# Small TensorE products grouped in a planned order: hybrid retention, hgrn2 and differential attention, two layers

## The chip, the cores and the metric

One Trainium2 chip, one of its cores. The metric is the device time of one execution in microseconds (us). The kernel before was run three times; the median is 1280.63 us.

## The reference

Two layers over 272 tokens (16 learned "meta" tokens and 256 of the input), width 1024, float32. Each layer normalizes the tokens, multiplies them by one wide matrix `w_in` and hands the columns to three branches: retention, hgrn2 and differential attention. Each branch output passes its own 1024 x 1024 matrix, is gated by a sigmoid and summed; `w_out` follows, then a feed-forward block with a three-tap convolution. Cut to what matters here:

```python
proj = (hn @ w_in).astype(F32)
rq, rk, rv, rg, hq, hf, hi, hg, dq, dk, dv, mg = jnp.split(proj, offs, axis=-1)
o_ret = retention(rq, rk, rv, rg, ...)        # 4 heads, s = (q k) * decay, o = s v, rms, * silu(rg)
o_hg  = hgrn2(hq, hf, hi, hg, lb, valid)      # 8 heads, a[q,k] = sum_d q k exp(cb_q - cb_k), o = a v
o_da  = diff_attention(dq, dk, dv, ...)       # 8 heads, w = softmax_0 - lam * softmax_1, o = w v
y = sum over the three of sigmoid(mg) * (branch @ w_branch)
h = h + y @ w_out
h = h + (silu(gate) * val) @ w_ffn_out        # gate, val from a convolution of h @ w_ffn_in
```

## The kernel before, in words

**The main products.** Tokens stand along the free dimension (272 columns; 258 in the last layer, where the first 14 meta tokens are needed for keys and values only), features along the partitions. A weight is split into two rounded halves, `whi` (ScalarE, ACT) and `wlo` (VectorE, DVE); so is the activation (`xh`, `xl`, or `b0hi`, `b0lo` and so on). Each 128 x 128 weight tile gives three products into the same PSUM accumulator, lines 942 to 944: whi x hi, whi x lo, wlo x hi. They are called main products below. Weights come in chunks of eight tiles (512 KB, tile `wraw`), issued by the SP queue.

**The order of the main products** is written out by hand: `ORDER` (line 63) lists pairs of column tiles, such as ("b0", 2), the third pair of the first branch product, 16 weight tiles. Marks stand between them: "+x" begins the work of a branch, "!x" is the point by which it has to be spread out, "*b0" splits a branch output into its rounded halves.

**The small products** are TensorE products of the branches, in full float32: for retention `s` (keys by queries) and `ro` (by values); for hgrn2 blocks of many tiny products (`lev`, `pm`, `far`), `px` (scores of the first chunk's keys with later queries, two heads to a bank), `ht` (the tail inside) and `ho` (outputs, three products a head: `at` by `vt`, `ax` by `vt`, `at` by `vt`); for attention `ds`, `wt`, `do`; and `vm`, which transposes the tails of the values. The profiler shows one such float32 product as two records (a transpose as one). They stand between main products on TensorE, which takes its instructions in order.

**The planner.** Nothing is issued while the kernel is traced; each operation goes to `_Plan.add` with an engine, an estimated cost, a key (a due time) and the tiles that it reads, writes and holds. `_Plan.order` (line 443) then plays the engines forward and, for each engine, takes the operation that can start first, the lower key first among equals (`rank`). A small product counts as ready only `SLACK` (0.6 us, line 343) after the planned end of what it needs on another engine. A PSUM buffer counts as free `FREE` + `SLACK` after its last planned use. The operations are issued in that order, and each waits on the chip for its real operands.

**PSUM.** Small products use two tags with two buffers each: "bank" (`bank`, line 721: `s`, `px`, `ht`, `lev`, `ds`, `wt`, `vm`) and "acc" (`acc_bank`, line 724: `ro`, `ho`, `do`, `far`, `pm`). The output of one hgrn2 head stays in its acc buffer through this chain: DVE adds the tail (`ho<-ho,am`), ACT squares it (`hsq`), GpSimd (POOL) sums over the partitions (`PARTITION_ALL_REDUCE hr<-hsq`), ACT makes the reciprocal root (`hr`), DVE multiplies (`ho<-ho,hr`), which reads the accumulator last.

Functions that the change touches: `tail_tokens` (line 1001, `vm`), `ret_head` (line 1081, `s`), `hg_heads` (line 1119, `px` at its end), `hg_outputs` (line 1359, `ht` and `ho`).

Of the kernel before, what the change touches and what calls it, by code (L numbers as in the profile page):

```python
# [20 lines left out]
P = 128  # L21
# [3 lines left out]
T = META + SEQ  # L25
# [31 lines left out]
def _pairs(name, lo, hi):  # L57
# [16 lines left out]
    + [("+hgob", 0)]  # L74
    + _pairs("dk", 0, 2)
    + [("+daa", 0), ("*b0", 0), ("!ret", 0), ("!hgob", 0)]
    + _pairs("dq", 2, 4) + _pairs("b0", 0, 4) + _pairs("dk", 2, 4) + _pairs("dv", 2, 4)
    + [("+dab", 0)]
    + _pairs("m1", 0, 4)
    + [("*b1", 0)]  # L80
    + _pairs("b1", 0, 3)
# [244 lines left out]


class _Op:
    __slots__ = ("engine", "run", "cost", "key", "func", "count", "tiles", "need", "after", "ready")

    def __init__(self, engine, run, cost, key, func, count):
        self.engine, self.run, self.cost, self.key, self.func, self.count = engine, run, cost, key, func, count
        self.tiles, self.need, self.after, self.ready = {}, 0, [], 0.0


class _Plan:
# [4 lines left out]
    LAG = {("act", "pe"): 0.35, ("dve", "pe"): 0.35, ("pool", "pe"): 0.35, ("pe", "act"): 0.22, ("pe", "dve"): 0.22, ("pe", "pe"): 0.0, ("sp", "act"): 0.0, ("sp", "dve"): 0.0}  # L341
    FREE = 0.3
    SLACK = 0.6
    SWITCH = 1.3
    SHARED = 0.35

# [96 lines left out]
    def order(self):  # L443

        times, mains = [m.key for m in self.main], set(self.main)
        for op in self.ops:
            i = bisect.bisect_right(times, op.key - EARLY) - 1
            if i >= 0 and op not in mains:
                self.queue(op, self.main[i])
        left = {}  # L450
        for op in self.ops:
            for n in op.tiles:
                left[n] = left.get(n, 0) + 1
        free = {tag: [0.0] * k for tag, k in self.room.items()}
# [12 lines left out]
        for op in self.ops:  # L467
            if op.need == 0:
                push(op)

        def start(op, t):

            want = {}
            for n in op.tiles:
                if n not in held:
                    want[self.tag[n]] = want.get(self.tag[n], 0) + 1
            first = [o for _, o in now["pe"] if o.count >= self.MANY and o.key < op.key]
            for tag, k in want.items():
# [11 lines left out]
        taken = shared = 0.0  # L490

        def comes(op):
            return op.count < self.MANY or (int(taken) - self.BEGIN.start) % self.PIECE < len(self.BEGIN)

        todo = len(self.ops)
        while len(out) < todo:
            best = None
            for e, t0 in engines.items():
                while later[e] and later[e][0][0] <= t0:
                    _, c, op = heapq.heappop(later[e])  # L500
                    now[e].append((c, op))
                found = None
                for c, op in now[e]:
                    t = start(op, t0) if comes(op) else None
                    if t is not None and (found is None or (t, rank(op), c) < found[:3]):
                        found = (t, rank(op), c, op)
                if later[e]:
                    t1 = later[e][0][0]
                    if found is None or t1 < found[0]:
                        found = (t1, 0.0, -1, None)  # L510
                if found is not None and (best is None or found[0] < best[0]):
                    best = found + (e,)
            if best is None:
                raise RuntimeError("no order: " + str([(e, [o.tiles for _, o in now[e]][:4]) for e in now]))
            t, _, c, op, e = best
            if op is None:
                engines[e] = t
                continue
            now[e].remove((c, op))
            cost = op.cost  # L520
            if op.func == "both" and shared > t:

                cost += min(shared - t, self.SHARED * cost)
            if op.func in self.SETS and self.SETS[op.func] != tables:
                tables = self.SETS[op.func]
                cost += self.SWITCH
                if tables == "le":
                    out.append(None)
# [12 lines left out]
            for n in op.tiles:  # L541
                left[n] -= 1
                if left[n] == 0:
                    free[self.tag[n]].append(done + self.FREE + (self.SLACK if self.tag[n] in ("bank", "acc") else 0.0))
            for o in op.after:
                o.need -= 1
                o.ready = max(o.ready, done + self.LAG.get((e, o.engine), self.CROSS) + (self.SLACK if o.engine == "pe" != e and o not in mains else 0.0))
                if o.need == 0:
                    push(o)
            if op.run is not None:  # L550
                out.append(op)
            else:
                todo -= 1
        return out
# [124 lines left out]
def _trace(ctx, tc, plan, a, depth, probe):  # L679
# [321 lines left out]
    def tail_tokens(tails):  # L1001

        pm = bank("vm")
        pe.transpose(pm[:, :P], tails, ident)
        vs = temp(P, "vs", 4)
        act.activation(vs, pm[:, :P], AF.Copy)
        return vs

    top, low = slice(0, P // 2), slice(P // 2, P)

# [35 lines left out]
    for li in range(depth):  # L1046
# [34 lines left out]
        def ret_head(hd):  # L1081
# [8 lines left out]
            parts = ((0, t0, t0, dec[:, t0:]), (P, P, T, dec[:, : P + TAIL]))  # L1090
            for k0, q0, at, _ in parts:
                pe.matmul(s1[:, at : at + T - q0], k[:, hd, k0 : k0 + P], q[:, hd, q0:], start=True, stop=True)
                plan.hold(a1)
            for _, q0, at, by in parts:
                tt(a1[:, at : at + T - q0], s1[:, at : at + T - q0], by, MUL)
# [23 lines left out]
        def hg_heads(b):  # L1119
# [229 lines left out]
                dve.copy_predicated(right(amh, s), split_q(lm), split_q(x))  # L1349

            ax = temp(4 * (P + TAIL), "ax", 1).rearrange("p (h t) -> p h t", h=4)
            for g in range(2):
                px = bank("px")[:, : 2 * (P + TAIL)].rearrange("p (h t) -> p h t", h=2)
                for j in range(2):
                    pe.matmul(px[:, j, :], k[:, 2 * g + j, :P], q[:, 2 * g + j, P:], start=True, stop=True)
                act.activation(ax[:, 2 * g : 2 * g + 2, :], px, AF.Copy)
            return lambda: hg_outputs(b, am, at, ax)

        def hg_outputs(b, am, at, ax):
            vt = st[f"hvt{b}"]  # L1360
            pt = bank("ht")[:, : 4 * TAIL]
            pe.matmul(pt, st[f"hvs{b}"], am, start=True, stop=True)
            inside = temp(4 * TAIL, "am", 3)
            act.activation(inside, pt, AF.Copy)
            for hd in range(4):
# [405 lines left out]
```

## Time and profile before

| what | value |
|---|---|
| three runs | 1281.78, 1280.63, 1280.21 us |
| median | 1280.63 us |
| the profiled execution | 1280.53 us |
| its span (first to last instruction) | 1278.7 us |
| time around the span | 1.8 us |
| TensorE matmul busy | 1270.1 us, 99% |
| DVE, ACT, POOL busy | 966.7, 863.9, 173.2 us |

PE is TensorE's matmul row, PEld its weight loads. Starts of TensorE instructions are recorded; the ends are modelled, and neighbours overlap, so distances between starts are what tells how long an instruction takes. A row of the timeline merges instructions of one kind that follow each other.

### The profile page before, as it was taken

The numbers are of one execution on the slowest core, as the hardware profiler recorded it, in microseconds if no ns is written. First come the engines' busy times: TensorE is split into PE (matmuls) and PEld (weight loads), VectorE is DVE, ScalarE is ACT, GpSimd is POOL, SyncE is SP. The second block draws the span as 40 slices with busy tenths as digits, with TensorE's granted clock in tenths as the row PEclk, the third lists the DMA queues.
The fourth block names the chain that finished last, engine by engine and source line by source line (L and its number), as shares of the span: only waits on it lengthen the run. The fifth ranks groups of instructions, "written<-read, shape, count | busy, mean of one in ns | idle before, by whom it ended". The sixth has DMA issues, their size and how long they took to land.

```text
span 1278.7 us, 26891 instructions
## 1 busy us (share of the span) xinstructions
PE 1270.1 (99%) x10777; PEld 1248.9 (98%) x10777; DVE 966.7 (76%) x1673; ACT 863.9 (68%) x1474; POOL 173.2 (14%) x158
## 2 busy tenths in 40 slices
PE   9999999999999999999999999999999999999998
PEld 8999999999999999999999999999999999999986
DVE  7685787697686789886575867886986867998853
ACT  6775585757787568776456655858568876787743
POOL 5000200123323030000020001012122310300000
PEclk9999999999999999999999999999999999999999
DMA  6764585545656555555556655755566566566663
GB/s 226 239 183 159 163 218 156 159 155 152 202 147 193 182 165 181 183 175 179 175 170 187 188 166 174 215 159 161 169 164 196 167 194 197 156 202 196 197 190 105
DMA packets 98892, 228.41 MB, mean 179 GB/s; under 512 B 45008, under 2 KB 45136, under 8 KB 98768
## 3 DMA queue, kind: packets, MB, share of 16 engines
q1 hardware_dynamic: 98480, 226.18, 58.2%
q8 instruction: 84, 1.38, 0.4%
q10 hardware_dynamic: 288, 0.52, 0.1%
q14 instruction: 40, 0.33, 0.1%
HBM read 216.19 MB, written 1.05 MB: 170 GB/s over the span
## 4 chain that ended last, share of the span: by engine, by line
PE 95%; DVE 2%; ACT 1%; issue 1%; DMA 1%; SPq 0%
PE main L944 28%; PE main L942 28%; PE main L943 28%; PE fo L1565 2%; PE fo L1567 2%; PE fo L1566 2%; PE ds L1430 1%; PE do L620 1%; PE ro L620 1%; PE ho L620 1%; PE lev L1155 1%; DVE wlo L620 1%; PE s L620 0%; DVE two_c L620 0%; DMA h<-in_h 0%
## 5 line engine op out<-in xcount | busy, mean ns | idle before, releaser
L942 PE MATMUL main<-xh,whi 128*128 128x272 f32 (+1 forms) x2368 | 686.0, 290 | 0.1
L944 PE MATMUL main<-xh,wlo 128*128 128x272 f32 (+1 forms) x2368 | 679.6, 287 | 1.4 <-DVE wlo L620 1.4
L943 PE MATMUL main<-xl,whi 128*128 128x272 f32 (+1 forms) x2368 | 670.6, 283 | 0.0
L620 DVE TENSOR_TENSOR wlo<-wraw,whi 128x1024 fp32r<-128x1024 f32 (+1 forms) x408 | 506.0, 1244 | 212.6 <-ACT whi L620 211.4
L620 ACT ACTIVATE whi<-wraw 128x1024 fp32r<-128x1024 f32 (+1 forms) x408 | 427.3, 1050 | 196.7 <-PE main L943 123.8
L943 PEld LDWEIGHTS main<-xl,whi 128*128 128x128 f32 x2368 | 449.5, 190 | 0.3
L942 PEld LDWEIGHTS main<-xh,whi 128*128 128x128 f32 x2368 | 445.6, 188 | 1.6 <-ACT whi L620 0.4
L944 PEld LDWEIGHTS main<-xh,wlo 128*128 128x128 f32 x2368 | 444.6, 188 | 2.3 <-DVE wlo L620 2.3
L620 POOL PARTITION_ALL_REDUCE hr<-hsq x36 | 72.0, 2024 | 170.5 <-ACT hsq L620 155.0
L620 POOL TENSOR_TENSOR y<-h,rstd 128x272 f32<-128x272 f32 x32 | 38.6, 1239 | 304.2 <-ACT rstd L620 304.2
L620 DVE SCALAR_TENSOR_TENSOR two_b<-u,small,two_b 128x256 f32<-128x256 f32 (+2 forms) x176 | 79.2, 493 | 0.1
L944 PE MATMUL main<-ghi,wlo 128*128 128x272 f32 x176 | 51.0, 290 | 0.0
L942 PE MATMUL main<-ghi,whi 128*128 128x272 f32 x176 | 50.8, 288 | 0.0
L943 PE MATMUL main<-glo,whi 128*128 128x272 f32 x176 | 50.2, 285 | 0.0
L620 ACT ACTIVATE two_b<-u,small 128x272 f32<-128x272 f32 (+1 forms) x88 | 48.4, 597 | 1.9 <-DVE glo L620 1.8
L620 ACT ACTIVATE u<-main 128x544 f32<-128x544 f32 (+1 forms) x40 | 24.4, 610 | 30.3 <-PE main L944 30.2
L942 PE MATMUL main<-b1hi,whi 128*128 128x272 f32 (+1 forms) x128 | 37.0, 289 | 0.0
L942 PE MATMUL main<-b0hi,whi 128*128 128x272 f32 (+1 forms) x128 | 36.8, 287 | 0.0
L944 PE MATMUL main<-yhi,wlo 128*128 128x272 f32 (+1 forms) x128 | 36.5, 286 | 0.0
L944 PE MATMUL main<-b2hi,wlo 128*128 128x272 f32 (+1 forms) x128 | 36.5, 285 | 0.0
L944 PE MATMUL main<-b0hi,wlo 128*128 128x272 f32 (+1 forms) x128 | 36.5, 285 | 0.0
L944 PE MATMUL main<-b1hi,wlo 128*128 128x272 f32 (+1 forms) x128 | 36.5, 285 | 0.0
(263 smaller groups left out, 1942.9 us busy)
## 6 DMA issues: line engine op xcount, KB each, us to landing
wraw<-in_w SPq DMA_DIRECT2D x402, 512.0 KB, 3.6
h<-in_h SPq DMA_DIRECT2D x4, 272.0 KB, 5.7
dec<-in_dec SPq DMA_DIRECT2D x2, 544.0 KB, 5.4
wraw<-in_w SPq DMA_DIRECT2D x4, 256.0 KB, 5.3
const<-in_const SPq DMA_DIRECT2D x1, 937.0 KB, 8.2
gain<-in_gl SPq DMA_DIRECT2D x1, 512.0 KB, 4.4
out<-y ACTq DMA_DIRECT2D x2, 256.0 KB, 2.7
out<-y SPq DMA_DIRECT2D x2, 256.0 KB, 2.7
```

Source lines behind the costliest of these rows:

```text
L620: self.plan.add(self.name, lambda: f(*args, **kw), cost, outs, ins, self._kind(method, args, ins), count)
L942: nc.tensor.matmul(o, wh, hi, start=first, stop=False)
L943: nc.tensor.matmul(o, wh, lo, start=False, stop=False)
L944: nc.tensor.matmul(o, wl, hi, start=False, stop=last)
L1155: nc.tensor.matmul(o, keys, x, start=True, stop=True)
L1430: nc.tensor.matmul(ss[m][:, at : at + nk], q[half, hd, q0 : q0 + P], k[half, hd, :nk], start=True, stop=True)
L1565: nc.tensor.matmul(o, gh, wh, start=False, stop=False)
L1566: nc.tensor.matmul(o, gl, wh, start=False, stop=False)
L1567: nc.tensor.matmul(o, gh, wl, start=False, stop=end)
```

## The change

Four things, all in what the planner is told or does.

1. In `ORDER`, the pairs 2 and 3 of the first branch product `b0` move behind `dk`, `dv` and the mark "+dab" (the start of the second half of attention).
2. The planner remembers whether TensorE's last operation was a small product (`visit`). If it was, a small product that can start at the same time goes ahead of any main product. If it wasn't, a small product with a `hold` may not start until `hold` us after it is ready. A main product behind a small one costs `TURN` = 0.09 us more in the plan.
3. `hold` is 8 us for `vm` and 2.5 us for `s` and `ht`.
4. The four products of `px`, and the six products of two heads of `ho`, are one entry of the plan each (`together`), issued one behind the other. Both accumulators of the two heads are taken by that entry.

```diff
-    + _pairs("dq", 2, 4) + _pairs("b0", 0, 4) + _pairs("dk", 2, 4) + _pairs("dv", 2, 4)
+    + _pairs("dq", 2, 4) + _pairs("b0", 0, 2) + _pairs("dk", 2, 4) + _pairs("dv", 2, 4)
     + [("+dab", 0)]
+    + _pairs("b0", 2, 4)
...
+    TURN = 0.09
...
                 for c, op in now[e]:
                     t = start(op, t0) if comes(op) else None
-                    if t is not None and (found is None or (t, rank(op), c) < found[:3]):
-                        found = (t, rank(op), c, op)
+                    if t is None:
+                        continue
+                    r = rank(op)
+                    if e == "pe" and op not in mains:
+                        if visit:
+                            r -= 1000.0
+                        else:
+                            t = max(t, op.ready + op.hold)
+                    if found is None or (t, r, c) < found[:3]:
+                        found = (t, r, c, op)
...
+            if e == "pe":
+                cost += self.TURN * (visit and op in mains)
+                visit = op not in mains
...
         pe.transpose(pm[:, :P], tails, ident)
+        plan.ops[-1].hold = 8.0
...
+    def together(calls, ins):
+        def run():
+            for o, x, y, first, last in calls:
+                nc.tensor.matmul(o, x, y, start=first, stop=last)
+
+        cost = sum(max(0.22, 4 * math.prod(c[0].shape[1:]) / 2312) for c in calls)
+        plan.add("pe", run, cost, [c[0] for c in calls], ins, count=4 * len(calls))
...
                 pe.matmul(s1[:, at : at + T - q0], k[:, hd, k0 : k0 + P], q[:, hd, q0:], start=True, stop=True)
+                plan.ops[-1].hold = 2.5
...
-            for g in range(2):
-                px = bank("px")[:, : 2 * (P + TAIL)].rearrange("p (h t) -> p h t", h=2)
-                for j in range(2):
-                    pe.matmul(px[:, j, :], k[:, 2 * g + j, :P], q[:, 2 * g + j, P:], start=True, stop=True)
+            pxs = [bank("px")[:, : 2 * (P + TAIL)].rearrange("p (h t) -> p h t", h=2) for _ in range(2)]
+            together([(pxs[hd // 2][:, hd % 2, :], k[:, hd, :P], q[:, hd, P:], True, True) for hd in hs], [k, q])
+            for g, px in enumerate(pxs):
...
             pe.matmul(pt, st[f"hvs{b}"], am, start=True, stop=True)
+            plan.ops[-1].hold = 2.5
...
-                o = acc_bank("ho")
-                ec = slice(hd * P, hd * P + P)
-                pe.matmul(o[:, t0:P], vt[:, 0, ec], at[:, hd, t0:P], start=True, stop=False)
-                pe.matmul(o[:, P:T], vt[:, 0, ec], ax[:, hd, :], start=False, stop=False)
-                pe.matmul(o[:, P:T], vt[:, 1, ec], at[:, hd, P:], start=False, stop=True)
+                if hd % 2 == 0:
+                    os = [acc_bank("ho") for _ in range(2)]
+                    calls = []
+                    for o, of in zip(os, (hd, hd + 1)):
+                        ec = slice(of * P, of * P + P)
+                        calls += [(o[:, t0:P], vt[:, 0, ec], at[:, of, t0:P], True, False),
+                                  (o[:, P:T], vt[:, 0, ec], ax[:, of, :], False, False),
+                                  (o[:, P:T], vt[:, 1, ec], at[:, of, P:], False, True)]
+                    together(calls, [vt, at, ax])
+                o = os[hd % 2]
```

More of the change, by code (lines that the diff above doesn't have):

```diff
@@ L328 @@
 class _Op:
-    __slots__ = ("engine", "run", "cost", "key", "func", "count", "tiles", "need", "after", "ready")
+    __slots__ = ("engine", "run", "cost", "key", "func", "count", "tiles", "need", "after", "ready", "hold")
     def __init__(self, engine, run, cost, key, func, count):
         self.engine, self.run, self.cost, self.key, self.func, self.count = engine, run, cost, key, func, count
-        self.tiles, self.need, self.after, self.ready = {}, 0, [], 0.0
+        self.tiles, self.need, self.after, self.ready, self.hold = {}, 0, [], 0.0, 0.0
 class _Plan:
@@ L490, in order @@
         taken = shared = 0.0
+        visit = True
         def comes(op):
@@ L1362, in hg_outputs @@
             pe.matmul(pt, st[f"hvs{b}"], am, start=True, stop=True)
+            plan.ops[-1].hold = 2.5
             inside = temp(4 * TAIL, "am", 3)
             act.activation(inside, pt, AF.Copy)
+            os = []
             for hd in range(4):
                 g = st["hg"][:, 4 * b + hd, t0:]
-                o = acc_bank("ho")
-                ec = slice(hd * P, hd * P + P)
-                pe.matmul(o[:, t0:P], vt[:, 0, ec], at[:, hd, t0:P], start=True, stop=False)
-                pe.matmul(o[:, P:T], vt[:, 0, ec], ax[:, hd, :], start=False, stop=False)
-                pe.matmul(o[:, P:T], vt[:, 1, ec], at[:, hd, P:], start=False, stop=True)
+                if hd % 2 == 0:
[8 more added lines that the diff above has]
+                o = os[hd % 2]
                 tt(o[:, 2 * P : T], o[:, 2 * P : T], inside[:, hd * TAIL : (hd + 1) * TAIL], ADD)
```

## The prediction, as put on record before the result

> **What bounds the kernel now.** I read the page first, then PE's waits, then PE's busy time by window, then the timeline around single small products.
>
> ```profile
> span 1278.7 us, 26891 instructions
> PE 1270.1 (99%) x10777; PEld 1248.9 (98%) x10777; DVE 966.7 (76%) x1673; ACT 863.9 (68%) x1474; POOL 173.2 (14%) x158
> PE 95%; DVE 2%; ACT 1%; issue 1%; DMA 1%; SPq 0%
> ```
>
> TensorE (PE) is busy for 99% of the span, and 95% of the chain that ended last is PE. Next, PE's waits (us in total, times, longest) and the stretch from 25 to 1208 us (us, then the busy time of PE, PEld, DVE, ACT, POOL, the granted clock, the DMA share and GB/s).
>
> ```profile
> PE main L944 <- DVE wlo L620: 1.4, 2, 0.9
> 25.00:1208.00 1183.00, 1182.71 (x10336) 1174.57 (x10335) 917.72 (x1617) 816.56 (x1406) 163.73 (x144) 1.00 0.59 179
> ```
>
> The one listed wait for operands is 1.4 us at the start of the run. Between 25 and 1208 us PE lacks 0.29 us of 1183, at the full clock (1.00). So no transfer and no chain on the other engines sets the end: the time is what PE's instructions take one behind another. The change leaves out no product, so it can save only (a) what it costs PE to turn from the main stream to a small product and back, and (b) the few short waits in which the stream stands before a small product. It can lose only by adding such waits.
>
> **The change, part by part.** The compiled order of PE's instructions has the same 10121 products in both kernels. In the old one the small products stand in 114 places between main products (I call each place a visit), in the new one in 89: 25 visits fewer. Of these 13 come from the outputs of hgrn2 (ho, 21 visits to 8), 3 from px (7 to 4), 5 from the transposes of the tails (vm), 4 from retention and the rest.
>
> *What is one visit worth?* The old trace holds the same products both alone and joined. Columns are the start, the time from the first start to the last end of the row's instructions, engine and line. First px: one pair of heads alone, then (after "...") both pairs in one visit.
>
> ```profile
> 114.95 0.29 PE L944 MATMUL main<-xh,wlo 128*128 128x272 f32 x1
> 115.08 0.65 PE L620 MATMUL px<-hq,hf 128*128 128x144 f32 x4
> 115.48 0.38 PE L942 MATMUL main<-xh,whi 128*128 128x272 f32 x1
> 115.70 0.29 PE L943 MATMUL main<-xl,whi 128*128 128x272 f32 x1
> 115.82 0.29 PE L944 MATMUL main<-xh,wlo 128*128 128x272 f32 x1
> 115.95 0.29 PE L942 MATMUL main<-xh,whi 128*128 128x272 f32 x1
> ...
> 203.78 0.29 PE L944 MATMUL main<-xh,wlo 128*128 128x272 f32 x1
> 203.91 1.14 PE L620 MATMUL px<-hq,hf 128*128 128x144 f32 x8
> ...
> 205.26 0.28 PE L942 MATMUL main<-xh,whi 128*128 128x272 f32 x1
> ```
>
> The starts are to be read, since the ends are modelled. Undisturbed main products start 0.125 us apart (115.70, 115.82, 115.95). From 114.95 to 115.95 stand four main products and one px pair: 1.00 - 4 x 0.125 = 0.50 us for the visit. From 203.78 to 205.26 stand four main products and both pairs: 1.48 - 0.50 = 0.98 us. Two single visits cost 1.00, one joint visit 0.98: **0.02 us for one visit less**.
>
> Now one head's three products of ho: together at 134.82; then the first (128 columns) and the second (144) each in a visit of its own.
>
> ```profile
> 134.82 0.29 PE L944 MATMUL main<-xh,wlo 128*128 128x272 f32 x1
> 134.95 0.38 PE L620 MATMUL ho<-at,vt 128*128 128x128 f32 x2
> 135.16 0.41 PE L620 MATMUL ho<-ax,vt 128*128 128x144 f32 x2
> 135.41 0.41 PE L620 MATMUL ho<-at,vt 128*128 128x144 f32 x2
> ...
> 136.03 0.28 PE L942 MATMUL main<-xh,whi 128*128 128x272 f32 x1
> ...
> 151.99 0.29 PE L944 MATMUL main<-xh,wlo 128*128 128x272 f32 x1
> ...
> 152.71 0.29 PE L942 MATMUL main<-xh,whi 128*128 128x272 f32 x1
> ...
> 153.70 0.29 PE L944 MATMUL main<-xh,wlo 128*128 128x272 f32 x1
> ...
> 154.44 0.29 PE L942 MATMUL main<-xh,whi 128*128 128x272 f32 x1
> ```
>
> Together: 136.03 - 134.82 - 0.50 = 0.71 us. Alone: 152.71 - 151.99 - 0.50 = 0.22 and 154.44 - 153.70 - 0.50 = 0.24; the third, of the second's size, is taken at 0.24 too: 0.70. Two visits less save -0.01, that is nothing.
>
> So three dropped visits saved 0.01 us in all; I take 0.007 us a visit for 0.02/3 with the loss put down to rounding. The ends are -0.005 (half of the -0.01) and 0.02. For 25 visits: **-0.2 us, from +0.1 to -0.5**.
>
> What would speak for more is in the px rows. The first main product behind a visit holds its successor off by 0.22 (115.48 to 115.70) and not 0.125: 0.095 us that look like a price of turning back, about the new TURN of 0.09. But the product before it started early: the last px passes are still being worked off when the main product's start is recorded. Counted from the main product ahead of the visit to the fourth behind, this 0.095 is the tail of px itself, and a joint visit pays it between its own products.
>
> The Trainium skill, "TensorE: Matmul & The Clock Gate", section "Step-by-step: what each phase is for", says that a single isolated matmul cannot hide its drain of some 128 cycles, while in a stream the drain of one lies beside the fill of the next. If a visit's edge counted as isolated, an estimate by that page would be 128 cycles at 2.4 GHz, 0.053 us a visit, and 1.3 us for 25. The ho rows (0.71 joined, 0.70 apart) show no such term.
>
> *Waits that the change may remove.* Two visits of the old run found their operands late. The rows are the DVE instruction that the first waited for, and the weight load of each small product with the idle time before it.
>
> ```profile
> 262.58 0.43 DVE L620 TENSOR_TENSOR ho<-ho,hr 128x272 f32<-128x272 f32 x1
> 263.13 0.30 PEld L620 LDWEIGHTS ho<-at,vt 128*128 128x128 f32 x2 [0.33 <-issue]
> ...
> 280.86 0.30 PEld L620 LDWEIGHTS wt<-const,wts 128*128 128x128 f32 x2 [0.33 <-issue]
> ```
>
> Both stand 0.33 us: 0.66 us. The plan's guess of the other engines was too early by so much. In the new order both places are dealt anew, so I count **-0.66 us**.
>
> *Waits that it may add.* A pair of heads of ho now takes both acc banks. The second pair must wait until DVE has read both heads of the first (ho<-ho,hr), and the main products queue in order behind it. The old run has two places where two heads end together. The last product of the two, and DVE's second read:
>
> ```profile
> 127.21 0.41 PE L620 MATMUL ho<-at,vt 128*128 128x144 f32 x2
> 135.73 0.43 DVE L620 TENSOR_TENSOR ho<-ho,hr 128x272 f32<-128x272 f32 x1
> ...
> 887.77 0.41 PE L620 MATMUL ho<-at,vt 128*128 128x144 f32 x2
> 897.28 0.41 DVE L620 TENSOR_TENSOR ho<-ho,hr 128x258 f32<-128x258 f32 x1
> ```
>
> From the last product's recorded start to the end of that read: 136.16 - 127.21 = 8.95 us and 897.69 - 887.77 = 9.92 us; counted from when PE goes on, some 0.15 us later, 8.8 and 9.8. In the new order 75, 90, 81 and 78 main products stand between the first and the second pair (layer 0 first and second half, layer 1 first and second half). At 0.125 us that is 9.4, 11.2, 9.6 and 9.8 us (the third at 0.125 x 258/272, since its products have 258 columns). The first has 0.6 us in hand, the last none. So I expect one wait of the size seen, 0.33 us, there. The plan also adds 0.09 us to its own PE time at each visit, which by the sum above is not spent: PE comes to the next product earlier than planned, by 0.09 for each visit in between, and eats into the 0.6 us of SLACK. For that I take a second wait of 0.33. New waits: **+0.66 us**, from 0 to six of them, 2.0 us.
>
> *The hold* of 8 us (vm) and 2.5 us (s, ht) delays only products that nothing waits for at once; hidden behind main products. If that cover is gone, each costs one wait, within the six. *The split of b0* moves two pairs, each 16 weight tiles of three products (16 x 3 x 0.125 = 6 us), behind dk and dv, with their four weight DMAs. The DMA queue of SP follows the same stream with as many transfers, none of them ahead of an earlier need; the DVE products y<-main,m move along. The second half of attention may start up to 12 us earlier. It is off the path (PE waits for nothing there), so 0; without cover it would be a wait in the range above.
>
> **Sum**, against the profiled execution: 1280.53 us (span 1278.7 and 1.8 around it) - 0.2 - 0.66 + 0.66 = 1280.3 us. The median of the runs shown, 1280.63, is 0.1 us above that execution. I predict **1280.3 us**, no change that counts; 0.2% (2.6 us) is about what a measurement here can tell from none.
>
> **The rivals.** *Turning has its own price.* For it: the 0.095 us behind each visit, and the plan's TURN; against it, the px and ho sums. It would give 25 x 0.095 = 2.4 us, with the old waits gone 1280.53 - 2.4 - 0.66 = 1277.5 us, faster by 0.24%. The page named above would put a drain in its place.
>
> *The pair waits for its banks.* Mechanism: acc has two banks and the second ho pair needs both. If one more all-reduce stands ahead on POOL in the chain of the first pair, the chain grows by its length:
>
> ```profile
> 128.50 3.79 POOL L620 PARTITION_ALL_REDUCE hr<-hsq  x2 [15.32 <-ACT hsq L620]
> ```
>
> that is 1.9 us. With 8.8 us in the first three places and 9.8 in the last, the four chains take 10.7, 10.7, 10.7 and 11.7 us, against 9.4, 11.2, 9.6 and 9.8: PE waits 1.3 + 0 + 1.1 + 1.9 = 4.3 us. With both waits of old gone and the visits' 0.2 saved that is 1284.0 us, slower by 0.27%. It begins where the chain is longer than the main products between the pairs, and decides from 3.4 us of waits in all. For it: the last place has no margin. Against it: POOL is busy 14%, and its two all-reduces here ran one behind the other.
>
> That the change doesn't do what it says is excluded by the compiled order (114 to 89); that this is worth nothing is the forecast.
>
> **How the numbers follow.** Forecast 0.85, turning priced 0.07, pair waits 0.08. The forecast's own range: all of the best ends, 1280.53 - 0.5 - 0.66 = 1279.4; all of the worst, 1280.53 + 0.1 + 2.0 with the old waits kept = 1282.6. It holds 0.85, so it is the range, rounded to 1279.2 to 1282.6. Faster by over 0.2%: 0.07; within: 0.85; slower: 0.08.
>
> **What would show it.** Right: main products still 0.125 us apart, 89 visits, each joint ho visit of six products 2 x 0.71 = 1.4 us, and the span within 2 us. The turning rival would show a joint px visit well under 0.98 us or six ho products under 1.3. The bank rival would show idle time before the second ho pair's weight load, with DVE ho<-ho,hr just ended. The forecast is wrong if main products wait for weights or banks anywhere behind 25 us, or if their spacing changes.

## The result, and the profile after

The changed kernel takes 1283.88 us (median of 16 runs, 1281.94 to 1288.82); the kernel before took 1280.71 us beside it (16 runs, 1279.72 to 1281.78). The ratio is 1.0029 (of the means; the two medians alone give 1.0025), 95% interval 1.0022 to 1.0035: slower by 3.2 us, where no change was forecast. The traced execution of the changed kernel is the shortest of its 16 (1281.94 us), so its trace shows less of the loss than the median has.

The page of the kernel after, its busy time from 25 to 1208 us (columns as before), and PE's waits (us in total, times, longest):

```profile
span 1280.0 us, 26891 instructions
PE 1269.3 (99%) x10777; PEld 1248.2 (98%) x10777; DVE 964.9 (75%) x1673; ACT 867.6 (68%) x1474; POOL 177.1 (14%) x158
PE 94%; issue 2%; DVE 1%; POOL 1%; ACT 1%; DMA 0%; SPq 0%; POOLq 0%; DVEq 0%
```

```profile
25.00:1208.00 1183.00, 1180.54 (x10314) 1172.17 (x10314) 914.19 (x1614) 818.44 (x1403) 166.30 (x143) 1.00 0.61 179
```

```profile
PE do L634 <- issue: 1.2, 1, 1.2
PE wt L634 <- DVE wts L634: 1.0, 1, 1.0
PE warm L634 <- POOL ones_d L634: 1.0, 1, 1.0
PE main L958 <- DVE wlo L634: 0.7, 2, 0.5
PE main L956 <- ACT whi L634: 0.6, 1, 0.6
PE ro L634 <- DVE at L634: 0.2, 1, 0.2
```

The list of waits has three new rows, do, wt and ro: small products of attention and retention, none of them touched by the joint entries. In the long stretch PE now lacks 2.46 us of 1183, before it lacked 0.29. These columns count only idle time between modelled ends. A wait is better measured from starts: the time from the main product ahead of a place to the one behind it, less what the same small products take at undisturbed places. So measured, places with small products lose 0.78 us in the trace of before (ho 262.73 and wt 280.46 us) and 3.42 us in that of after: do 388 us 1.48, ro 846 and 854 us 0.52, wt 916 us 1.30, do 1019 us 0.12. Both old waits are gone. In the first 17 us, where the main products wait for their first weights, the traced run of after happens to lose 1.73 us and that of before 2.85; that makes up for 1.1 us, and the spans lie only 1.3 us apart.

What the two rivals needed isn't there. A joint px visit and a joint ho visit of the kernel after:

```profile
114.71 0.29 PE L958 MATMUL main<-xh,wlo 128*128 128x272 f32 x1
114.83 1.14 PE L1029 MATMUL px<-hq,hf 128*128 128x144 f32 x8
...
116.20 0.29 PE L956 MATMUL main<-xh,whi 128*128 128x272 f32 x1
```

```profile
122.28 0.29 PE L958 MATMUL main<-xh,wlo 128*128 128x272 f32 x1
122.40 0.38 PE L1029 MATMUL ho<-at,vt 128*128 128x128 f32 x2
...
124.21 0.29 PE L956 MATMUL main<-xh,whi 128*128 128x272 f32 x1
```

Four main products stand in each stretch (0.50 us): px takes 1.49 - 0.50 = 0.99 us (0.98 joined before), ho 1.93 - 0.50 = 1.43 us (2 x 0.71 forecast). No ho product of after waits, the second pairs included.

**How the wait at do 388 us comes about.** First SP's queue in the kernel before at this place (start, time up to the end of the row's last issue, instruction):

```profile
386.37 1.22 SPq L620 DMA_TRANSPOSE two_a<-two_b  x1
387.69 0.52 SPq L620 DMA_DIRECT2D wraw<-in_w  x1
391.43 1.22 SPq L620 DMA_TRANSPOSE two_a<-two_b  x1
```

Then the kernel after: SP, POOL, ACT, PE, each its own timeline, and the stretch from 387 to 389 us (its last columns are the clock, the DMA share and GB/s).

```profile
378.23 5.33 SPq L634 DMA_TRANSPOSE two_a<-two_b  x2
383.65 10.18 SPq L634 DMA_DIRECT2D wraw<-in_w  x5
```

```profile
379.06 3.26 POOL L634 COPY two_b<-two_a 128x512 uint16<-128x512 uint16 x1 [2.45 <-DVE two_a L634]
```

```profile
385.14 1.07 ACT L634 ACTIVATE wts<-two_a 128x768 uint16<-128x768 uint16 x1 [1.13 <-DMA two_a<-two_b]
388.14 1.06 ACT L634 ACTIVATE whi<-wraw 128x1024 fp32r<-128x1024 f32 x1 [1.93 <-DMA wraw<-in_w]
389.10 0.17 ACT L634 ACTIVATE dot<-do 128x16 f32<-128x16 f32 x1
...
389.47 0.17 ACT L634 ACTIVATE dot<-do 128x16 f32<-128x16 f32 x1
```

```profile
388.22 0.29 PE L958 MATMUL main<-xh,wlo 128*128 128x272 f32 x1
389.75 0.92 PE L634 MATMUL do<-wts,vt 128*128 128x272 f32 x4 [1.24 <-issue]
```

```profile
387.00:389.00 2.00, 1.51 (x13) 1.29 (x11) 0.00 (x0) 0.86 (x1) 0.00 (x0) 1.00 1.01 395
```

In before SP issued a weight load between the two transposes. In after they are adjacent; the second waits for POOL's copy, which ends at 382.32, and SP, which takes its instructions in order, issues no weight load from 378.23 to 383.65. The loads then come together (395 GB/s from 387 to 389 us). ACT stands idle 1.93 us for weights, splits them, and only then reads the two accumulators (`dot<-do`, the last at 389.47) that the next `do` needs. PE takes its instructions in order and stands until then.

**The wait at wt 916 us.** DVE in the kernel after, then PE; then the same two in the kernel before.

```profile
909.13 0.43 DVE L634 TENSOR_TENSOR ho<-ho,hr 128x258 f32<-128x258 f32 x1 [1.50 <-ACT hr L634]
...
917.50 0.23 DVE L634 TENSOR_SCALAR wts<-wts 128x16 f32<-128x16 f32 x1
```

```profile
916.55 0.28 PE L958 MATMUL main<-b0hi,wlo 128*128 128x258 f32 x1
917.88 0.41 PE L634 MATMUL wt<-const,wts 128*128 128x64 f32 x2 [1.05 <-DVE wts L634]
```

```profile
916.95 0.22 DVE L620 TENSOR_SCALAR wts<-wts 128x16 f32<-128x16 f32 x1
```

```profile
917.84 0.28 PE L944 MATMUL main<-b0hi,wlo 128*128 128x258 f32 x1
917.96 0.33 PE L620 MATMUL wt<-const,wts 128*128 128x64 f32 x2
```

Before, `wts` was ready 0.8 us ahead of its product. After, PE arrives 1.3 us earlier and DVE 0.55 us later: DVE lost 1.50 us waiting for the norm of a ho head and has worked without a gap since 909.13.

### The profile page after: what moved, and what is told of

Its sections match the earlier page's. It is cut to its first block, busy times and chain, and to the rows that moved or that the text cites. A ratio compares the mean times of both kernels' runs of the same rounds, so it can differ in the third digit from the quotient of the medians.

```text
span 1280.0 us, 26891 instructions
## 1 busy us (share of the span) xinstructions
PE 1269.3 (99%) x10777; PEld 1248.2 (98%) x10777; DVE 964.9 (75%) x1673; ACT 867.6 (68%) x1474; POOL 177.1 (14%) x158
## 3 DMA queue, kind: packets, MB, share of 16 engines
HBM read 216.19 MB, written 1.05 MB: 170 GB/s over the span
## 4 chain that ended last, share of the span: by engine, by line
PE 94%; issue 2%; DVE 1%; POOL 1%; ACT 1%; DMA 0%; SPq 0%; POOLq 0%; DVEq 0%
PE main L958 28%; PE main L956 28%; PE main L957 28%; PE fo L1597 2%; PE fo L1599 2%; PE fo L1598 2%; PE ds L1462 1%; PE do L634 1%; POOL hr L634 1%; PE ro L634 1%; PE ho L1029 1%; PE lev L1181 1%; PE s L634 0%; DMA h<-in_h 0%; PE px L1029 0%
## 5 line engine op out<-in xcount | busy, mean ns | idle before, releaser
L634 POOL PARTITION_ALL_REDUCE hr<-hsq x36 | 75.8, 2131 | 164.8 <-ACT hsq L634 148.6
L634 POOL MEMSET at<- 128x1088 f32 x4 | 4.0, 1009 | 247.6 <-PE far L1181 124.8
```

The source lines that it names most:

```text
L634: self.plan.add(self.name, lambda: f(*args, **kw), cost, outs, ins, self._kind(method, args, ins), count)
```

## The experiments

The theory after the result: a visit costs nothing, and all of the loss is waits in front of small products, because PE runs ahead of a plan that counts a cost (TURN) it doesn't pay, and eats up SLACK. Rivals: visits have a price after all; or the split of b0, through SP's queue, is what costs. The parts of the change are called split, TURN, joint (px and ho), preference and hold. All ratios are to the kernel before with 95% interval.

| kernel | split, TURN, joint, preference, hold | visits | do 388 | ro 846 to 857 | wt 916 | elsewhere | time, us | ratio |
|---|---|---|---|---|---|---|---|---|
| before | - - - - - | 114 | 0 | 0 | 0 | 0.78 | 1280.71 | 1 |
| after | S T J P H | 89 | 1.48 | 0.52 | 1.30 | 0.12 | 1283.88 | 1.0029 (1.0022 to 1.0035) |
| e4 | S T J P H | 89 | 2.66 | 1.35 | 1.29 | 0 | 1284.95 | 1.0032 (1.0020 to 1.0043) |
| e1 | S - - - - | 114 | 0 | 0 | 0 | 0.98 | 1281.98 | 1.0011 (1.0002 to 1.0019) |
| e5 | - T - - - | 121 | 0 | 0 | 0 | 0.96 | 1280.50 | 1.0000 (0.9991 to 1.0009) |
| e17 | S T - - - | 121 | 0.97 | 0 | 0 | 1.05 | 1282.87 | 1.0018 (1.0008 to 1.0027) |
| e12 | - T J - - | 110 | 0 | 0.11 | 0 | 0.63 | 1280.69 | 1.0000 (0.9991 to 1.0009) |
| e2 | - T J P H | 91 | 0 | 0.74 | 1.29 | 1.04 | 1281.77 | 1.0009 (1.0000 to 1.0018) |
| e3 | S - J P H | 84 | 0 | 0 | 0.29 | 0.22 | 1280.02 | 0.9996 (0.9987 to 1.0005) |
| e8 | S, TURN -0.03, J P H | 87 | 0 | 0 | 0.52 | 0.89 | 1281.02 | 1.0006 (0.9998 to 1.0015) |
| e13 | S T J P - | 88 | 2.73 | 0.46 | 1.29 | 0.77 | 1282.86 | 1.0024 (1.0013 to 1.0036) |
| e14 | S T J - H | 95 | 4.31 | 0 | 1.01 | 1.29 | 1285.84 | 1.0040 (1.0027 to 1.0052) |
| e16 | S T - P H | 96 | 1.09 | 0.93 | 0 | 2.48 | 1282.63 | 1.0019 (1.0010 to 1.0027) |

The waits are of one traced run each, in us, counted to the main product behind the place. In e14 the granted clock fell to half at the end of the wait at do (0.79 from 393 to 395 us, 0.50 from 395 to 397): 3.1 of its 4.31 us go by before `do` starts, and the other 1.2 are `do` itself at that clock.

**e1: the split alone, in the kernel before.**

```diff
-    + _pairs("dq", 2, 4) + _pairs("b0", 0, 4) + _pairs("dk", 2, 4) + _pairs("dv", 2, 4)
+    + _pairs("dq", 2, 4) + _pairs("b0", 0, 2) + _pairs("dk", 2, 4) + _pairs("dv", 2, 4)
     + [("+dab", 0)]
+    + _pairs("b0", 2, 4)
```

> The kernel before with the split of b0 alone (part 1 of the change); planner, px and ho as before, 114 visits as before. Split theory (the loss comes from moving dv and the start of attention's second half ahead of two b0 pairs: its transposes stand next to each other on the SP queue and hold the weight DMAs behind them): slower than before by 2 to 4 us, with waits of over 1 us before a small product of attention. Plan theory (the loss comes from TURN and the preference in a visit, which let PE arrive before its operands): 1280.7 us, no difference to before. Grouping theory (pairs of ho need both banks): also 1280.7 us.

Measured 1281.98 us, 1.5 us over the kernel before. The trace has small waits (ho, ds, wt near 264 to 280 us, 0.16 at 1018 us). Main products lose 3.5 us in it: some 2.3 in the first 17 us, less than in the trace of before, and 1.2 at 970 and 1009 us, where before has nothing; the longer of the two is a wait for DVE (0.57 us of idle time, `dm`). The span is only 0.6 us longer, so a good half of the 1.5 us isn't explained by it, and neither theory's time came. It has no wait at do 388 us: the split alone doesn't make it.

**e2: the kernel after with the old ORDER** (the lines above, undone).

> The changed kernel with the old ORDER (b0 in one piece), all else changed: TURN, preference, hold, joint px and ho. Split theory: back at 1280 to 1281 us. Plan theory: stays at about 1283.5 us. Grouping theory: stays at about 1283.5 us, with idle time before second pairs of ho.

Measured 1281.77 us. The wait at do 388 us is gone; those at ro and wt stay, and one of 1.04 us stands at do 1030. The time lies between those of the two theories.

**e3: the kernel after with TURN = 0.**

```diff
-    TURN = 0.09
+    TURN = 0.0
```

> The changed kernel with TURN = 0, all else changed. Plan theory: PE no longer arrives early, waits before small products go from 3.4 us to under 1 us, time 1280 to 1281 us. Split theory: stays slower than before by 2 to 4 us, for the transposes stand as close on the SP queue.

Measured 1280.02 us, with 84 visits. At do and ro nothing is left, at wt 0.29 of 1.30 us. Of all single parts this is the one whose removal takes the loss away.

**e4: the kernel after once more, unchanged.**

> The changed kernel once more, nothing edited, for a second profile. All theories: 1283 to 1285 us. If the waits follow from the order of the queues they stand at the same three products (do at 388 us, ro at 846 us, wt at 917 us), with sizes that differ by some tenths; if they are chance, at others. Where the time is above 1284 us the granted clock should fall below 0.999 behind the longest wait.

Measured 1284.95 us; the traced run (1285.59 us) waits 5.29 us in all and keeps a clock of 1.00, where a lower one was expected. So the places are the same from run to run and the lengths aren't, at do above all.

**e5: TURN alone, in the kernel before.**

```diff
+    TURN = 0.09
...
+            if e == "pe":
+                cost += self.TURN * (visit and op in mains)
+                visit = op not in mains
```

> The kernel before with one thing of the change alone: the plan adds TURN = 0.09 us to a main product behind a small one. No preference, no hold, no joint px or ho, old ORDER. Plan theory (PE runs ahead of the plan by 0.09 us a visit and stands before products whose operands are late): slower than before by 1 to 5 us, with waits of 0.5 us and more before ro, wt or do. If TURN does harm only together with the joint products: 1280 to 1281 us.

Measured 1280.50 us. TURN alone does no harm, so "TURN eats SLACK" isn't enough as a theory; it needs another part beside it.

**e6: the kernel before with small products taken apart**: wherever two follow each other in the planned order and the next main product may stand between them, it is put there. That was done at 81 places; some of these only moved the edge of a visit, and the trace has 191 visits, counted as the 114 of before are: 77 more.

> The kernel before, its finished plan edited: wherever two small products follow one another, one triple of main products from behind is pulled in between, if its operands allow; 81 visits more (114 to 195), the same products, the other engines' orders untouched. By the sum of the prediction (0.007 us a visit, between -0.005 and 0.02): +0.6 us, between -0.4 and +1.6, apart from new waits. If turning has a price of 0.095 us: +7.7 us, 1288 us.

Measured 1282.13 us, ratio 1.0014 (1.0005 to 1.0023). The span is 1.4 us longer, of which 0.98 are more waits (1.76 in all, the largest 0.67 at ro 866 us) and about 0.4 main products that stand late at 336 and 412 us: nothing is left for 77 more visits. The Trainium skill, "TensorE: Matmul & The Clock Gate", section "Step-by-step: what each phase is for", has an isolated matmul unable to hide a drain of some 128 cycles; if each visit's edge counted as isolated, an estimate from that (0.053 us a visit) would give 4.1 us here, and no run shows that term.

**e7: the kernel after with four small products put a few main products later** in the planned order (do 24, wt 12, ro 6 and 9; two `s` products that share a place with one ro move along), nothing else.

```diff
+    LATER = {"do_353": 8, "wt_691": 4, "ro_616": 3, "ro_615": 2}
```

> The changed kernel, its finished plan edited at four products alone: do (wait at 388 us) stands 24 main products later, wt (916 us) 12 later, two of ro (844 to 849 us) 6 and 9 later; all else as changed, with the drift of TURN in it. If the waits at these products are the loss: they go, and the time falls by 2.5 to 4 us to 1280.5 to 1282 us. If PE's being early is the cause and the waits only its outlet: part of the loss returns as waits at the next small products, time 1282 to 1283.5 us.

Measured 1280.33 us, ratio 1.0001 (0.9992 to 1.0010). PE's waits in its trace:

```profile
PE main L1000 <- DVE wlo L676: 1.6, 3, 0.9
PE warm L676 <- POOL ones_d L676: 1.0, 1, 1.0
PE main L998 <- ACT whi L676: 0.6, 2, 0.5
```

The rows for do, wt and ro are gone and no row came in their place. By starts, 0.87 us of small waits stand elsewhere (ro 854, ds 919, do 1020 us), about as much as the 0.78 of before. So waits at these four places are the whole loss; with them out, 89 visits run as fast as 114.

**e8: the kernel after with TURN = -0.03.**

> The changed kernel with TURN = -0.03 in place of 0.09: the plan has PE a little early, so that operands get margin. Plan theory: no wait over 0.3 us, time 1279.3 to 1280.3 us, at or below that with TURN = 0. If the margin doesn't matter and each plan has its own chance waits: anywhere from 1279.5 to 1283 us.

Measured 1281.02 us: no wait at do and ro, but 0.68 at wt 281 and 0.52 at wt 916 us. Less TURN than none isn't better.

**e9: one weight load put ahead of the first of the two adjacent transposes** on SP.

```diff
+        out.insert(turn, out.pop(load))
```

> The kernel after, with one issue of SP moved in the planned order: the weight DMA of chunk 116 (the branch product's pair behind the place where b0 was split) goes ahead of the first of the two transposes, between which the kernel after has no weight load; nothing else moves. Theory (SP's order): the two transposes one behind the other hold the weight loads, three of them then land together at 387 to 389 us, ACT splits them ahead of reading the small product's bank, and do at 388 us waits 1.5 us (2.7 us in the second run of the same kernel). With the load ahead the wait at do 388 us falls under 0.5 us; the other waits (ro 846, wt 916, do 1019) stay, some 2 to 3.4 us; time 1.0 to 2.2 us under the kernel after, 1281.7 to 1283. Rival (the wait comes from the plan's drift alone, whatever SP does): the wait at 388 us stays at 1.5 to 2.7 us and the time at 1284 to 1285.

Measured 1283.18 us, ratio 1.0020 (1.0011 to 1.0028). The wait at do did not fall: 1.67 us. SP, ACT and PE there:

```profile
382.46 2.55 SPq L642 DMA_TRANSPOSE two_a<-two_b  x2
```

```profile
387.11 1.96 ACT L642 ACTIVATE wts<-two_a 128x768 uint16<-128x768 uint16 x2 [3.35 <-DMA two_a<-two_b]
```

```profile
388.31 0.92 PE L642 MATMUL do<-wts,vt 128*128 128x272 f32 x4 [1.43 <-ACT wts L642]
```

The load put ahead pushed the first transpose from 378.23 to 382.46 us; now ACT waits 3.35 us for the transposes, and `do` for their result. The expectation failed. What stands is that one in-order queue carries both the weights and attention's transposes, and at this place each makes the other late; which of them comes first decides only who is named in the wait.

**e10 and e11: more margin.** The kernel after with SLACK 1.6 (e10), and with TURN 0 and SLACK 1.2 (e11).

```diff
-    SLACK = 0.6
-    TURN = 0.09
+    SLACK = 1.2
+    TURN = 0.0
```

> The kernel after with SLACK 1.6 instead of 0.6 us, TURN kept at 0.09. Theory (margin): the lateness of DVE against the plan grows by about 1 us at ro 846 and wt 916 through TURN and the new plan, and a wait is that lateness less SLACK; 1 us more of SLACK takes the waits at wt, ro and do away: under 1 us of waits before small products, span 1278 to 1279.5, time 1280 to 1281. Rival (each plan draws its waits by chance, the margin does not govern them): waits stay between 0.5 and 5 us at whatever places, time anywhere from 1280 to 1285, at least 2 us of waits as likely as not.

> The kernel after with TURN 0 and SLACK 1.2 us: the joint entries, the preference, the holds and the split stay (83 places with small products between main products). Theory: a place with small products costs PE nothing beyond their own passes, so nothing is to be had by fewer of them; what is to be had is the waits of the kernel before (0.8 us) and no more: 1279.3 to 1280.3 us, ratio 0.9990 to 1.0000. Rival (a place has its price of 0.095 us): 31 fewer give 2.9 us, 1277.5 us, ratio 0.9977.

e10: 1280.45 us, 0.9998 (0.9989 to 1.0007); 0.45 us of waits (wt 980 us), and 1.0 us of a main product at 950 us. One us more of SLACK takes the waits at do, ro and wt away with TURN still there. In e10 and e11 a weight load stands between the two transposes again (0.53 us from 387.10 and from 387.16), so at do the larger margin can't be told from the changed order on SP. e11: **1279.11 us, 0.9989 (0.9980 to 0.9998)**, faster than both kernels, with 83 visits and no wait before any small product. All of PE's waits in e11:

```profile
PE main L958 <- DVE wlo L634: 1.2, 2, 0.7
PE warm L634 <- POOL ones_d L634: 1.0, 1, 1.0
```

**e12: px and ho joint and TURN, without the rest.**

> The kernel before with two parts of the change: px and ho joint (one entry each) and TURN 0.09; no preference for small products, no hold, b0 not split. TURN alone ran at the time of the kernel before, with waits of 1.0 us in all. Theory A (TURN together with the joint pairs, which begin the chain of two heads at once, is enough to make DVE late against the plan by 1 us or more at ro 846 and wt 916): waits of 1 to 2 us there, time 1281.3 to 1282.5. Theory B (it needs the preference and the holds, which put the small products in groups and so DVE's work behind them): waits there under 0.5 us, time 1280 to 1280.9. In both, no wait near 388 us, since b0 is not split.

Measured 1280.69 us: theory B. TURN with the joint entries makes none of the waits.

**e13, e14, e16: the kernel after without the holds, without the preference, without the joint entries.**

> The kernel after without the holds (vm, s and ht may follow as soon as they are ready); preference, TURN 0.09, joint entries and the split stay (88 places with small products between main products). Theory H (the holds gather the small products and so DVE's work behind them): waits before ro, wt and do under 1.2 us in all, 1280.5 to 1281.5 us. Theory P (the preference together with TURN makes them): 2.5 to 5 us of waits, 1282.5 to 1285 us.

> The kernel after without the preference (a small product that can follow another one has no priority over main products); holds, TURN 0.09, joint entries and the split stay (95 places). Theory P: waits before ro, wt and do under 1.2 us in all, 1280.5 to 1281.5 us. Theory H: 2.5 to 5 us of waits, 1282.5 to 1285 us. If both this and the run without holds lose their waits, either needs the other; if neither does, it is TURN with the split.

> The kernel after with px and ho as separate entries as before; preference, holds, TURN 0.09 and the split stay (96 places). If the joint entries are part of the cause: waits under 1.5 us in all, 1280.5 to 1281.5 us. If not: the waits at do 388, ro 846 and wt 916 us stay, 2.5 us or more in all, 1282.5 to 1285 us. I expect the second, since no wait in the kernel after stands at ho or px.

All three keep more than 4 us of waits, so none of these parts is the cause alone; both theories of e13 and e14 fall for do 388, which leaves the last sentence of e14's expectation: TURN with the split. The table sorts it by place. In it, do 388 waits in every kernel that has both split and TURN 0.09 (e17 below among them), and in no other. These six are also the ones whose two transposes stand side by side on SP (5.32 or 5.33 us for both); in e1, e3 and e8, with the split but without TURN 0.09, a weight load of 0.53 us stands between them. ro 846 to 857 waits 0.46 to 1.35 us where TURN 0.09 and the preference are together, and at most 0.11 us elsewhere. wt 916 waits 1.0 to 1.3 us where TURN 0.09, the joint entries and the preference or the hold are together, 0.29 and 0.52 us with TURN 0 or below, and not at all without the joint entries.

e13 also shows why single runs lie so far apart. Its windows around the wait and five rows of PE:

```profile
389.00:393.00 4.00, 1.51 (x11) 1.24 (x10) 1.18 (x1) 2.27 (x6) 0.75 (x1) 1.00 0.51 204
393.00:397.00 4.00, 4.00 (x23) 4.00 (x22) 2.81 (x5) 2.51 (x8) 3.06 (x2) 0.57 0.51 143
```

```profile
389.55 0.29 PE L956 MATMUL main<-xh,wlo 128*128 128x272 f32 x1
392.33 0.92 PE L632 MATMUL do<-wts,vt 128*128 128x272 f32 x4 [2.49 <-issue]
...
394.03 0.43 PE L954 MATMUL main<-xh,whi 128*128 128x272 f32 x1
394.26 0.43 PE L955 MATMUL main<-xl,whi 128*128 128x272 f32 x1
```

After 2.49 us without work the granted clock is 0.57 from 393 to 397 us: 16 main products stand 0.227 us apart (394.03, 394.26) instead of 0.125, that is 1.6 us more. The three runs of e13 with a clock of 0.997 or 0.998 took 1286.36 to 1286.64 us, the five with 0.999 or 1.0 took 1282.12 to 1283.17. In the kernel after, five of the six runs above 1285 us have a clock of 0.998 or less, and the ten below have 0.999 or 1.0; the wait at do 388 is the likely reason there too, though no trace of such a run of after was taken, and of the three runs of e4 above 1285 us only one has a clock under 0.999. The Trainium skill, "TensorE: Matmul & The Clock Gate", section "What's actually happening", has the clock fall to half after an idle window of about 3.4 us and rise again after as much work. Half speed and its length (393.5 to 397 us) agree with that; the idle time needed here was shorter: this wait is 2.73 us by starts, and one of 2.66 us in e4 left the clock at 1.00.

**e15: the kernel before with SLACK 1.2. e17: split and TURN in the kernel before. e18: split and SLACK 1.2 in the kernel before.**

> The kernel before with SLACK 1.2 instead of 0.6 us, nothing of the change. Theory (a place with small products costs nothing, waits are all there is): its two waits (0.8 us) go and it runs as the changed kernel with TURN 0 and SLACK 1.2 does, 1278.8 to 1280 us, ratio 0.9985 to 0.9995. Rival (31 places fewer are worth something after all): it stays at 1280 to 1281 us, 1 us or more above that one.

Measured 1296.70 us, ratio 1.0132 (1.0116 to 1.0147), far off what was expected. Its two longest rows of waits:

```profile
PE main L942 <- ACT b2hi L620: 10.5, 2, 6.5
PE main L943 <- DVE b2lo L620: 1.7, 2, 1.1
```

In the kernel before with more SLACK, attention ends after the main products that need it (`b2hi`), by 4.0 and 6.5 us, and the main products behind each of these waits stand 0.227 and 0.215 us apart for a while. That it is every small product being put later that makes the chain so long is argued, not shown. Margin has a price, and "waits are all there is" says nothing of where a plan puts them.

> The kernel before with two parts of the change: b0 split in the order and TURN 0.09; no joint entries, preference or holds (121 places with small products between main products). Its planned issue order on SP has no weight load between the last two of these transposes of the first layer, as in the kernel after and in the three variants of it that waited at do. Theory (TURN with the split is the cause at do 388; the rest is needed for ro and wt): a wait of 1 to 4.5 us at do near 390 us, under 0.6 us at ro 846 and wt 916; time 1281.5 to 1284. If ro and wt wait as well: 2.5 us or more in all, 1283 to 1285.5, and TURN with the split is the whole cause. If do does not wait: the holds, the preference or the joint entries are needed after all, any two of them.

Measured 1282.87 us. do waits (0.97 us), ro and wt don't. SP and PE:

```profile
379.32 5.33 SPq L626 DMA_TRANSPOSE two_a<-two_b  x2
384.74 9.10 SPq L626 DMA_DIRECT2D wraw<-in_w  x5
```

```profile
390.32 0.92 PE L626 MATMUL do<-wts,vt 128*128 128x272 f32 x4 [0.72 <-issue]
```

It is the picture of the kernel after with two of its five parts: split and TURN together are enough for this wait.

> The kernel before with b0 split and SLACK 1.2; no TURN, joint entries, preference or holds (115 places). In the kernel before with SLACK 1.2, main products waited 4.0 and 6.5 us for the output of attention (ACT b2hi). Theory (the split lets the second half of attention begin earlier and gives this time back): no such wait, 1278.8 to 1280 us. Rival (the joint entries, preference and holds are what shortens the chain): waits for b2hi of 2 us or more at 412 and 1051 us, 1285 us or more.

Measured 1283.20 us, ratio 1.0020 (1.0011 to 1.0028): between the two. Its rows for attention's output:

```profile
PE main L944 <- DVE b2lo L621: 0.9, 1, 0.9
PE main L943 <- ACT b2hi L621: 0.2, 1, 0.2
```

These waits shrink from 12.2 to 1.1 us, so most of e15's loss is given back by the split, but the time of e11 (1279.11) takes the joint entries, the preference and the holds as well. Which of these does it wasn't tried.

## Why the prediction was wrong, point by point

**Right.** *PE bounds everything*: main products still stand 0.125 us apart. Take from each span the waits before small products and what main products lose (start, late weights and accumulators, `b2hi`, half clock): 1274.4 to 1275.4 us is left in all 20 traces, with 83 to 191 visits. *25 visits are worth 0.2 us*: e6 bounds a visit to next to nothing, e7 and e3 show no gain from 25 or 30 fewer. *Both old waits go*: they did, 0.78 us by starts. *The turning rival* (1277.5) had its test, px under 0.98 us, and px took 0.99. *The bank rival* had its test, idle time before the second ho pair, and there is none; its 1284.0 us lies near the result for a reason that isn't its own. *The hold costs nothing*: without it (e13) the waits are as long.

**Wrong: the term of the new waits**, +0.66 us, "from 0 to six of them, 2.0 us". They are 3.42 us in the shortest run and 5.29 in e4's trace. The step that failed is the size: each new wait was given the 0.33 us of the two old ones. An old wait shows only what the old plan's errors were, and its margin had been enough nearly everywhere. The mechanism was named ("PE comes to the next product earlier than planned" and "eats into the 0.6 us of SLACK"), but priced as one wait of 0.33; at wt 916 taking TURN away removes 1.0 us of 1.30 (e3). The other wait was put at the last ho pair, where none came. By the prediction's own numbers, 0.09 us a visit, twelve visits in a row are worth more than a us, nearly twice SLACK; that sum was not made. But TURN alone was harmless (e5), so the full size also needs the parts that regroup small products. Why, beyond the table's combinations, stays open: the runs show that TURN 0.09 is needed for these waits, while how far PE runs ahead of its plan was not measured. None of the signs that the prediction set for being wrong names what came, small products that wait for their operands.

**Wrong: the split at 0**, because SP's queue has "none of them ahead of an earlier need" and "It is off the path". The transfers were counted and their neighbours weren't looked at. With TURN the split lets two transposes stand side by side on SP, the second of which waits for POOL; weights, ACT's reading of the accumulators and `do` queue behind (1.0 to 2.7 us in five of the six traces of the table, and 3.1 us before `do` starts in e14). e2 and e3 take away either part and the wait with it. That SP's order alone is the lever was tried and isn't so (e9).

**Not foreseen**: a wait of this length can also cost clock, 1.6 us more in e13. The lower end of the range is 1279.4 by its own sum and was put down as 1279.2; nothing hangs on it.

## What to carry to other kernels

When a planner's cost is raised, first measure that the chip pays it: a cost that isn't paid can let the engine run ahead of the plan, and then every margin along the way has to cover the sum since the last place where they met (here argued: taking TURN away took the waits away, the lead itself was not measured). Price a new wait from what lies behind it in the engines' queues, not from the length of old waits, and look at which instructions become neighbours in an in-order DMA queue, even if their number stays the same. And regrouping that saves no time of its own can still be worth keeping for the freedom it gives to a larger margin: e11 beats both kernels, while the same margin cost the kernel before 16 us.

## What the runs showed of the hardware that was not expected

- Going from a float32 small product to the main stream and back costs PE next to nothing: 77 more such places left no time beyond waits (e6).
- A wait of 2.73 us (by starts) was followed by some 3.5 us at half the granted clock in e13, and one of 2.66 us in e4 was not; in e14 the clock halved at the end of a wait of 3.1 us.
- The same POOL copy (128 x 512, uint16) took 0.61 us and, 3 us later, 3.26 us in the kernel after. The long one ends at 382.32 us, 0.47 behind the two `wlo` splits that DVE ran beside it (379.49 to 381.85 us). In e3, with one `wlo` beside it, it took 2.13 us and ended 0.48 us behind that one; in e5 it was 2.13 and 0.48 us too. So it looks as if the copy waits for DVE, which was not tested.

```profile
375.99 0.61 POOL L634 COPY two_b<-two_a 128x512 uint16<-128x512 uint16 x1 [7.06 <-issue]
```
